# A recurrent mixer in which the token shift of V is given out behind Q

## The chip, the cores and the metric

The kernel runs on one core of a Trainium2 chip. Its time is the device time of one execution in microseconds. A core has five engines that run their own lists of instructions side by side: TensorE (PE, with PEld for its weight loads), VectorE (DVE), ScalarE (ACT), GpSimd (POOL) and SyncE (SP). Each engine takes its list strictly in order, and an instruction waits by semaphores for what other engines and DMAs have to deliver. DMAs are issued from SP and from ACT; in the profile such an issue has the engine's name with a q (SPq, ACTq).

## The reference

The model is a trunk of residual sub-layers over 256 tokens of width 1024: SwiGLU, mixer, SwiGLU, in two kinds of layer. The change lies in the first kind's mixer, whose recurrent half has 8 heads of 64. Cut to what the change touches:

```python
proj = h @ w_in
p = proj[..., :COLS_RWKV]
p_prev = jnp.pad(p, ((0, 0), (1, 0), (0, 0)))[:, :-1]
p = p + shift_mu * (p_prev - p)                 # token shift of r, k, v and the low-rank inputs
r, k, v, d_w, d_a, d_g = split_cols(p, [...])
w_log = -jax.nn.softplus(-(decay_base + jnp.tanh(d_w) @ decay_up)) - 0.5
decay = jnp.exp(-jnp.exp(w_log))
a = jax.nn.sigmoid(iclr_base + d_a @ iclr_up)
kk = k * k_k;  kk = kk * rsqrt(sum(kk * kk))    # per head
k = k * (1.0 + (a - 1.0) * k_a)
# S_t = S_{t-1} diag(w_t) - (S_{t-1} kk_t)(kk_t*a_t)^T + v_t k_t^T ;  y_t = S_t r_t
y = rwkv7_scan(r, decay, k, v, kk, a)
y = group_norm(y)                               # per head: mean and variance over 64
glu = c_val * jax.nn.sigmoid(c_gate)            # the other half: a convolution of 31 taps
return concat([(y + bonus) * g, silu(layer_norm(conv(glu)))]) @ w_out
```

## The kernel before, in words

The program is one core's list of stages: SwiGLU, the recurrent mixer, two SwiGLUs, an attention mixer, a SwiGLU. Tokens stand in two tiles of 128 (t = 0 and 1). All products with weights run in three passes: a page of weights (128x1024) is loaded by SP (`raw`, L68), ACT casts it to `whi` (L100), and VectorE, or GpSimd for some pages, subtracts to get `wlo` (L101). The product's three passes are the lines L340 and L354 on PE. SP loads pages ahead into a ring of 10 buffers, so a page's subtraction also frees a buffer for the next load.

The recurrent mixer is written as sub-steps, functions in a table `f`, that are called in the order of the string `ORDER` (L22), "VLDKPvQkRIBCcbA2S". A tile framework then puts the instructions on the engines, taking them by the order in which they were given out and by its own estimate of when they become ready; so the string moves what it names, and the framework moves neighbours. What the sub-steps are, with the names that the rows use:

- V (`values`): the product for V. ACT writes it to `pv` (L619) and copies it, shifted by one token, into `prev` by DMAs from ACT's queue (L622). v (`m["rest"]`, L628): the same for the second tile, and `shift_values`.
- `shift_values`: for each tile t, GpSimd mixes in the shifted token (L632, L633, L634, 128x512 each), VectorE sums over the 64 of each head and scales (L636, L637, written to the small tile `misc`), and GpSimd subtracts that mean (L640, `vz`, 64x512, two for each tile).
- L and D: the low-rank inputs (`lora`), the gates `sg` and `ic` (sigmoids on ACT), the decay scan on VectorE (L684, `dc`), then GpSimd's `epx` (L686) and ACT's exponentials `ep`, `epx` (L689, L687).
- K, P, k: k with its shift (`shifted`: VectorE L645 `n`, ACT L648, VectorE L649) and what is made of it, `bk` (L700, L703, L726) and `ur` (L697).
- Q (`qmats`): PE multiplies `ur` and `bk` head by head, and VectorE writes the masked and scaled result in 16 instructions (L740).
- I (`invert`): Q goes out to DRAM and comes back with another layout (DMAs L750, L756), VectorE inverts the small triangular blocks (L759, L760, then multiply L775, L778 and sum L780 in three rounds), and the inverse goes out and back (`dg`, `G`, L785, L788).
- R: r with its shift (L645, L648, L649), `ur` from r (L797), and GpSimd's `sq` (L803). C (`glu`): the gated value `cv` (L858), the gate `z` (L863 on VectorE, L864 on ACT), `glu` (L869, L871). A: products of r and k, `ak` and `ar` (L828, L831), behind which PE starts the sequential part (L590).

VectorE, GpSimd, ACT and SP keep their lists in the order that the framework chose; nothing overtakes.

Of the kernel before, what the change touches and what calls it, by code (L numbers as in the profile page):

```python
# [12 lines left out]
ALU = mybir.AluOpType  # L13
PSUM = bass.MemoryType.PSUM
P = 128
D = 1024
# [2 lines left out]
TAG = dict(sq8="y2", qn="yc", gz="z", fz="tmp", fe="c16", fl="lora", fc="n", fraw="restart", pt="yb", y="muv",  # L19
           cb="ur", cbm="bk", gt="sg", qt="ic", kt="k", v="vz", y0="ar")  # L20

ORDER = "VLDKPvQkRIBCcbA2S"  # L22

NRAW, NWEIGHT, NAHEAD = 10, 8, 8

# [69 lines left out]
class Kernel:  # L95
# [470 lines left out]
    def mixer_a(self, j, rstd, nxt, then):  # L566
        nc, W, a = self.nc, self.w, self.a
        V = nc.vector
# [15 lines left out]
        m = {}  # L584

        def abank():
            return self.abank(3 if m.get("busy") else 4)

        def mm(out, lhsT, rhs, start=True, stop=True):
            return nc.tensor.matmul(out, lhsT=lhsT, rhs=rhs, start=start, stop=stop, skip_group_check=True)  # L590
# [17 lines left out]
        def values():  # L608


            vz = m["vz"] = [half(self.page("vz")) for _ in range(2)]
            pv, prev = m["v"], _ = half(self.page("pv")), half(self.page("prev"))
            W.upto(("av",))
            with self.tc.issue_after(self.pow.ins):
                nc.gpsimd.memset(prev[0:1, 0, :], 0.0)

            def product(t):
                ps = self.xunit(("av",), t)
                nc.scalar.activation(pv[:, t, :], ps, AF.Copy, scale=rstd[t])  # L619

                for a, b in ((0, 112), (112, P - 1)):
                    nc.scalar.dma_start(out=prev[a + 1:b + 1, t, :], in_=pv[a:b, t, :])  # L622
                if t == 0:
                    nc.scalar.dma_start(out=prev[0:1, 1, :], in_=pv[P - 1:P, 0, :])

            product(0)
            m["rb"] = self.across(rstd)
            m["rest"] = lambda: (product(1), shift_values(vz, pv, prev))  # L628

        def shift_values(vz, pv, prev):  # L630
            for t in range(2):
                nc.gpsimd.tensor_tensor(out=prev[:, t, :], in0=prev[:, t, :], in1=pv[:, t, :], op=ALU.subtract)  # L632
                nc.gpsimd.tensor_tensor(out=prev[:, t, :], in0=prev[:, t, :], in1=muv, op=ALU.mult)  # L633
                nc.gpsimd.tensor_tensor(out=pv[:, t, :], in0=prev[:, t, :], in1=pv[:, t, :], op=ALU.add)  # L634
                v8 = self.small("v8", 8)
                V.tensor_reduce(out=v8, in_=h8(pv[:, t, :]), axis=AX.X, op=ALU.add)  # L636
                V.tensor_scalar(out=v8, in0=v8, scalar1=1.0 / 64, scalar2=None, op0=ALU.mult)  # L637
                for c in range(2):
                    cs = slice(64 * c, 64 * c + 64)
                    nc.gpsimd.tensor_tensor(out=h8(vz[t][cs, c, :]), in0=h8(pv[cs, t, :]), in1=v8[cs].unsqueeze(2).broadcast_to([64, 8, 64]), op=ALU.subtract)  # L640
# [87 lines left out]
        def qmats():  # L728
            Q = m["Q"] = blk(self.page("Q"))
            bk, ur, nn = m["bk"], m["ur"], m["nn"]  # L730
            for t in range(2):
                pss = [abank()[:, 0:256].rearrange("p (g x) -> p g x", x=64) for _ in range(2)]
                for g in range(4):
                    for c in range(2):
                        for hp in range(2):
                            b, o = 64 * hp, 64 * (c ^ hp)
                            z = 1 + (1 - (c ^ hp))
                            mm(pss[hp][o:o + 64, g, :], bk[g // 2][b:b + 64, g % 2, t, z, :], ur[g // 2][b:b + 64, g % 2, t, z, :])
                for h in range(8):
                    V.scalar_tensor_tensor(out=Q[:, t, h, :], in0=pss[h % 2][:, h // 2, :], scalar=nn[:, t, h:h + 1], in1=self.tri[:, 0:64], op0=ALU.mult, op1=ALU.mult)  # L740

        def invert():

# [238 lines left out]
        def state():  # L982
# [4 lines left out]
            for ch in range(4):  # L987
# [35 lines left out]
                if c == 1:  # L1023
# [11 lines left out]
                    ts = slice(t * P, (t + 1) * P)  # L1035
                    self.split(self.xth[:, 0:4, ts], self.xtl[0][:, :, ts], tp.rearrange("p (g t) -> p g t", t=P))

        f = {"V": values, "v": lambda: m["rest"](), "L": lora, "K": keys, "D": decay, "P": prep, "k": kprep, "Q": qmats, "I": invert, "R": receptance, "A": amats,
             "B": kback, "C": glu, "2": doubling, "b": bonus, "c": conv, "S": state}
        for z in ORDER:  # L1040
            f[z]()
# [9 lines left out]
    def plan(self, stages):  # L1051
        W, a = self.w, self.a
        flat = lambda ap: ap.rearrange("p k f -> p (k f)")
        for st in stages:
# [17 lines left out]
            if st == "A":  # L1072
                for name in [n for z in ORDER for n in dict(V=["alora", "av"], K=["ak"], R=["ar"], C=["acv", "acg"]).get(z, [])]:
                    if name == "av":
# [154 lines left out]
```

## Time and profile before

| | us |
|---|---|
| median of 3 runs | 1127.58 (1126.9 to 1128.02) |
| profiled execution, own time | 1126.15 |
| profiled execution, span of the core | 1124.4 |
| PE busy in the span | 1082.3 (96%) |
| VectorE busy | 657.7 (58%) |
| ACT busy | 545.7 (49%) |
| GpSimd busy | 232.7 (21%) |

The span is the stretch from the first to the last instruction of the profiled execution; 1.75 us of its own time lie around it. The recurrent mixer's sub-steps lie between about 205 and 370 us of the span. PE is busy nearly everywhere; behind the first of the page's 40 slices (28.1 us each) the lowest is the one of 281 to 309 us, with 7 tenths for PE and 7 for its clock. The granted clock stands as a share of TensorE's full speed.

### The profile page before, as it was taken

To read this page: it belongs to the slowest core of one execution; us is meant where nothing else is said; L and a number is where in the kernel's file an instruction comes from. 1 tells how busy PE (TensorE), PEld (TensorE's weight loads), DVE (VectorE), ACT (ScalarE), POOL (GpSimd) and SP (SyncE) were. 2 spreads that over 40 slices of the span, in tenths; PEclk is the share of its full clock that TensorE was granted. 3 is DMA by queue.
4 is the path that set the end of the run, shared out by engine and by line. 5 is a ranking of instruction groups with operands and counts; after the bars stand their busy time and mean duration, and the time that the engine had idled before them with its cause. 6 is when DMAs were issued, how large, how long until landed. Compare 5 with 4: busy or idle time off the path is not lost.

```text
span 1124.4 us, 17702 instructions
## 1 busy us (share of the span) xinstructions
PE 1082.3 (96%) x7021; PEld 950.2 (85%) x7021; DVE 657.7 (58%) x1041; ACT 545.7 (49%) x876; POOL 232.7 (21%) x164
## 2 busy tenths in 40 slices
PE   7999999999799899999989999999999989999997
PEld 5899988779688779999878999988887868999986
DVE  4565661598874566557444655836666665555722
ACT  7444543572302564446354544644666945444611
POOL 5200005454700160000070000001564541000000
PEclk9999999999799999999999999999999999999999
DMA  9766784155631146547455655734273563665400
GB/s 358 252 211 188 235 291 160 56 177 157 159 110 38 59 166 246 215 185 272 155 183 162 194 188 184 235 127 150 92 284 112 189 188 112 208 187 187 149 1 38
DMA packets 66633, 192.84 MB, mean 172 GB/s; under 512 B 18520, under 2 KB 20216, under 8 KB 66550
## 3 DMA queue, kind: packets, MB, share of 16 engines
q1 hardware_dynamic: 56698, 189.75, 50.7%
q10 hardware_dynamic: 9852, 1.96, 0.9%
q8 instruction: 55, 0.90, 0.3%
q14 instruction: 28, 0.23, 0.1%
HBM read 187.86 MB, written 2.92 MB: 170 GB/s over the span
## 4 chain that ended last, share of the span: by engine, by line
PE 88%; DVE 4%; ACT 3%; POOL 2%; DMA 2%; issue 1%; ACTq 0%; DVEq 0%; SPq 0%; POOLq 0%
PE gu L354 32%; PE acc L265 21%; PE gu L225 15%; PE gu L340 6%; PE acc L590 5%; PE acc L372 3%; PE gu L590 1%; DVE x L150 1%; DVE wlo L101 1%; PE tr L160 1%; POOL p L486 1%; PE tr L245 1%; ACT whi L100 1%; DMA raw<-in_wgt_dram 1%; PE tr L508 1%
## 5 line engine op out<-in xcount | busy, mean ns | idle before, releaser
L100 ACT CAST whi<-raw 128x1024 fp32r<-128x1024 f32 x294 | 302.2, 1047 | 212.8 <-PE gu L354 114.3
L101 DVE TENSOR_TENSOR wlo<-raw,whi 128x1024 fp32r<-128x1024 f32 x248 | 310.5, 1260 | 145.6 <-ACT whi L100 122.7
L354 PE MATMUL gu<-xth,whi 128*128 128x256 f32 x1104 | 313.5, 284 | 0.9 <-DVE misc L810 0.6
L354 PE MATMUL gu<-xth,wlo 128*128 128x256 f32 x1104 | 313.5, 284 | 0.0
L354 PE MATMUL gu<-xl,whi 128*128 128x256 f32 x1104 | 312.8, 284 | 0.0
L354 PEld LDWEIGHTS gu<-xth,whi 128*128 128x128 f32 x1104 | 212.2, 192 | 4.4 <-issue 0.8
L354 PEld LDWEIGHTS gu<-xth,wlo 128*128 128x128 f32 x1104 | 212.2, 192 | 2.4
L354 PEld LDWEIGHTS gu<-xl,whi 128*128 128x128 f32 x1104 | 212.1, 192 | 0.8 <-issue 0.7
L101 POOL TENSOR_TENSOR wlo<-raw,whi 128x1024 fp32r<-128x1024 f32 x46 | 112.2, 2466 | 311.5 <-PE gu L225 142.0
L265 PE MATMUL acc<-whi,ht 128*128 128x512 f32 x576 | 168.0, 393 | 0.0
L115 POOL TENSOR_TENSOR misc<-misc 128x1 f32<-128x1 f32 (+1 forms) x36 | 31.4, 872 | 484.4 <-DVE misc L132 382.3
L265 PEld LDWEIGHTS acc<-whi,ht 128*128 128x128 f32 x576 | 104.0, 189 | 18.3
L265 PE MATMUL acc<-wlo,ht 128*128 128x512 f32 x288 | 89.9, 392 | 0.0
L236 DVE TENSOR_TENSOR h<-gu,h 128x256 f32<-128x256 f32 x88 | 36.8, 419 | 77.7 <-ACT h L232 74.2
L225 PE MATMUL gu<-whi,xth 128*128 128x512 f32 x160 | 63.6, 401 | 1.6 <-ACT whi L100 1.6
L225 PE MATMUL gu<-wlo,xth 128*128 128x512 f32 x160 | 63.6, 399 | 0.5 <-DVE wlo L101 0.5
L265 PEld LDWEIGHTS acc<-wlo,ht 128*128 128x128 f32 x288 | 53.9, 188 | 11.8
L225 PE MATMUL gu<-whi,xl 128*128 128x512 f32 x160 | 63.4, 401 | 0.4 <-DVE xl L165 0.4
L234 DVE TENSOR_TENSOR h<-gu,misc 128x256 f32<-128x256 f32 x56 | 23.7, 423 | 65.7 <-PE gu L354 65.6
L232 ACT ACTIVATE h<-gu,misc 128x256 f32<-128x256 f32 x32 | 15.1, 474 | 73.1 <-PE gu L225 39.9
L340 PE MATMUL gu<-whi,xl 128*128 128x512 f32 x112 | 44.9, 401 | 1.1 <-DVE xl L165 0.9
L340 PE MATMUL gu<-whi,xth 128*128 128x512 f32 x112 | 45.1, 403 | 0.7 <-ACT xth L164 0.7
(259 smaller groups left out, 1521.0 us busy)
## 6 DMA issues: line engine op xcount, KB each, us to landing
raw<-in_wgc_dram SPq DMA_DIRECT2D x112, 512.0 KB, 4.3
raw<-in_wd_dram SPq DMA_DIRECT2D x88, 512.0 KB, 4.5
raw<-in_wgt_dram SPq DMA_DIRECT2D x64, 512.0 KB, 4.8
raw<-in_cin_dram SPq DMA_DIRECT2D x24, 512.0 KB, 4.6
raw<-in_ain_dram SPq DMA_DIRECT2D x18, 512.0 KB, 4.3
raw<-in_aout_dram SPq DMA_DIRECT2D x8, 512.0 KB, 4.9
raw<-in_cgate_dram SPq DMA_DIRECT2D x8, 512.0 KB, 4.7
raw<-in_cout_dram SPq DMA_DIRECT2D x8, 512.0 KB, 5.8
```

Of the source, the lines that this page charges most:

```text
L100: self.nc.scalar.copy(out=hi, in_=raw)
L101: (engine or self.nc.vector).tensor_tensor(out=lo, in0=raw, in1=hi.bitcast(F32), op=ALU.subtract)
L115: self.pow = self.nc.gpsimd.tensor_tensor(out=out, in0=v, in1=self.mhalf[:, :n], op=ALU.pow)
L225: nc.tensor.matmul(ps, lhsT=l, rhs=r[:, k % 2], start=n == 0, stop=n == 23)
L232: nc.scalar.activation(sl, ps[:, 0:256], AF.Silu, scale=rstd[u[2]])
L234: nc.vector.tensor_tensor(out=z, in0=ps[:, 0:256], in1=self.rb, op=ALU.mult)
L236: nc.vector.tensor_tensor(out=h, in0=ps[:, 256:512], in1=sl, op=ALU.mult)
L265: mm = nc.tensor.matmul(out, lhsT=l, rhs=r, start=u[1] == 0 and i + n == 0, stop=u[1] == NB - 1 and i * 3 + n == 5)
L340: self.nc.tensor.matmul(ps, lhsT=l, rhs=r[:, k % 2], start=n == 0, stop=n == 23)
L354: self.nc.tensor.matmul(ps[:, j * 256:(j + 1) * 256], lhsT=l, rhs=r, start=n == 0, stop=n == 23)
L372: self.nc.tensor.matmul(accs[t][c], lhsT=l, rhs=r[:, 0, c * 512:(c + 1) * 512], start=k == ks[0] and n == 0, stop=k == ks[7] and n == 2)
L590: return nc.tensor.matmul(out, lhsT=lhsT, rhs=rhs, start=start, stop=stop, skip_group_check=True)
```

## The change

A new letter s, the shift of V, comes behind Q in the order, and v keeps only the second tile's product with its DMAs. The shift is wrapped in `issue_after` on the last of VectorE's 16 operations for Q. That edge orders instructions of one engine only: VectorE's L636 and L637 of both tiles have to stand behind Q in VectorE's list, while GpSimd's list gets no such edge. From L634 on all line numbers rise by 5.

```diff
--- before.py
+++ after.py
@@ -19,7 +19,7 @@
 TAG = dict(sq8="y2", qn="yc", gz="z", fz="tmp", fe="c16", fl="lora", fc="n", fraw="restart", pt="yb", y="muv",
            cb="ur", cbm="bk", gt="sg", qt="ic", kt="k", v="vz", y0="ar")
 
-ORDER = "VLDKPvQkRIBCcbA2S"
+ORDER = "VLDKPvQskRIBCcbA2S"
 
 NRAW, NWEIGHT, NAHEAD = 10, 8, 8
 
@@ -625,9 +625,14 @@
 
             product(0)
             m["rb"] = self.across(rstd)
-            m["rest"] = lambda: (product(1), shift_values(vz, pv, prev))
+            m["rest"], m["shift"] = lambda: product(1), lambda: shift_values(vz, pv, prev)
 
         def shift_values(vz, pv, prev):
+
+            with self.tc.issue_after(m["last_q"].ins):
+                shift_behind(vz, pv, prev)
+
+        def shift_behind(vz, pv, prev):
             for t in range(2):
                 nc.gpsimd.tensor_tensor(out=prev[:, t, :], in0=prev[:, t, :], in1=pv[:, t, :], op=ALU.subtract)
                 nc.gpsimd.tensor_tensor(out=prev[:, t, :], in0=prev[:, t, :], in1=muv, op=ALU.mult)
@@ -737,7 +742,7 @@
                             z = 1 + (1 - (c ^ hp))
                             mm(pss[hp][o:o + 64, g, :], bk[g // 2][b:b + 64, g % 2, t, z, :], ur[g // 2][b:b + 64, g % 2, t, z, :])
                 for h in range(8):
-                    V.scalar_tensor_tensor(out=Q[:, t, h, :], in0=pss[h % 2][:, h // 2, :], scalar=nn[:, t, h:h + 1], in1=self.tri[:, 0:64], op0=ALU.mult, op1=ALU.mult)
+                    m["last_q"] = V.scalar_tensor_tensor(out=Q[:, t, h, :], in0=pss[h % 2][:, h // 2, :], scalar=nn[:, t, h:h + 1], in1=self.tri[:, 0:64], op0=ALU.mult, op1=ALU.mult)
 
         def invert():
 
@@ -1035,7 +1040,7 @@
                     ts = slice(t * P, (t + 1) * P)
                     self.split(self.xth[:, 0:4, ts], self.xtl[0][:, :, ts], tp.rearrange("p (g t) -> p g t", t=P))
 
-        f = {"V": values, "v": lambda: m["rest"](), "L": lora, "K": keys, "D": decay, "P": prep, "k": kprep, "Q": qmats, "I": invert, "R": receptance, "A": amats,
+        f = {"V": values, "v": lambda: m["rest"](), "s": lambda: m["shift"](), "L": lora, "K": keys, "D": decay, "P": prep, "k": kprep, "Q": qmats, "I": invert, "R": receptance, "A": amats,
              "B": kback, "C": glu, "2": doubling, "b": bonus, "c": conv, "S": state}
         for z in ORDER:
             f[z]()
```

VectorE, the stretch from `ur` to the first operations for Q. `ur<-k` and `bk` are what PE multiplies for Q, `tr` their sums of squares, `r` the start of sub-step R, `misc<-pv` the mean of V's second tile. Before:

```order
L697 SCALAR_TENSOR_TENSOR ur<-k,cst,epx 128x2x128 x4
L703 TENSOR_TENSOR bk<-bk,dc 128x4x128 x2
L101 TENSOR_TENSOR wlo<-raw,whi 128x1024
L722 TENSOR_TENSOR k<-k,ic 128x1024
L645 TENSOR_TENSOR n<-gu,misc 128x512
L101 TENSOR_TENSOR wlo<-raw,whi 128x1024 x2
L726 TENSOR_TENSOR bk<-k,dc 128x4x2x64 x2
L715 TENSOR_SCALAR misc<-tr 64x16 x2
L649 SCALAR_TENSOR_TENSOR r<-n,cst,r 128x255 x2
L636 TENSOR_REDUCE misc<-pv 128x8
L716 RECIPROCAL misc<-misc 128x16
L797 TENSOR_TENSOR ur<-r,ep 128x2x2x64 x2
```

The 16 operations of Q follow (with one L637 ahead of them and one `wlo` ahead of the last). Now:

```order
L702 SCALAR_TENSOR_TENSOR ur<-k,cst,epx 128x2x128 x4
L708 TENSOR_TENSOR bk<-bk,dc 128x4x128 x2
L720 TENSOR_SCALAR misc<-tr 64x16 x2
L727 TENSOR_TENSOR k<-k,ic 128x1024
L101 TENSOR_TENSOR wlo<-raw,whi 128x1024
L721 RECIPROCAL misc<-misc 128x16
L101 TENSOR_TENSOR wlo<-raw,whi 128x1024
L731 TENSOR_TENSOR bk<-k,dc 128x4x2x64 x2
L745 SCALAR_TENSOR_TENSOR Q<-acc_2377,misc,cst 128x64 x3
```

Gone from ahead of Q are not only the sum of V, but also `n`, `r` and `ur` of sub-step R, one `wlo` of three, and the `wlo` that stood inside Q.

VectorE again, from the last operations for Q to the first step of the inversion (`inv<-inv`), whose operand comes back from DRAM. Before:

```order
L101 TENSOR_TENSOR wlo<-raw,whi 128x1024
L740 SCALAR_TENSOR_TENSOR Q<-acc_2418,misc,cst 128x64
L645 TENSOR_TENSOR n<-gu,misc 128x512
L101 TENSOR_TENSOR wlo<-raw,whi 128x1024
L649 SCALAR_TENSOR_TENSOR r<-n,cst,r 128x255 x2
L797 TENSOR_TENSOR ur<-r,ep 128x2x2x64 x2
L101 TENSOR_TENSOR wlo<-raw,whi 128x1024
L858 TENSOR_TENSOR cv<-gu,misc 128x512
L101 TENSOR_TENSOR wlo<-raw,whi 128x1024
L759 TENSOR_TENSOR inv<-inv,c_2608 128x256
```

Now:

```order
L745 SCALAR_TENSOR_TENSOR Q<-acc_2404,misc,cst 128x64
L641 TENSOR_REDUCE misc<-pv 128x8 x2
L650 TENSOR_TENSOR n<-gu,misc 128x512
L101 TENSOR_TENSOR wlo<-raw,whi 128x1024
L642 TENSOR_SCALAR misc<-misc 128x8
L101 TENSOR_TENSOR wlo<-raw,whi 128x1024
L642 TENSOR_SCALAR misc<-misc 128x8
L654 SCALAR_TENSOR_TENSOR r<-n,cst,r 128x255 x2
L101 TENSOR_TENSOR wlo<-raw,whi 128x1024
L802 TENSOR_TENSOR ur<-r,ep 128x2x2x64
L764 TENSOR_TENSOR inv<-inv,c_2608 128x256
L650 TENSOR_TENSOR n<-gu,misc 128x512
```

Both sums of V stand directly behind Q. The first half of r stands between Q and the inversion, and r's second half (`n`, two L654, two L802), one L802 of the first half, both `cv` and four `wlo` now stand behind the inversion's first step, where one `cv` and two `wlo` stood.

GpSimd, from the shift of V's first tile to `sq`, before:

```order
L632 TENSOR_TENSOR prev<-prev,pv 128x512
L633 TENSOR_TENSOR prev<-prev,muv 128x512
L634 TENSOR_TENSOR pv<-prev,pv 128x512
L101 TENSOR_TENSOR wlo<-raw,whi 128x1024
L640 TENSOR_TENSOR vz<-pv,misc 64x512 x2
L101 TENSOR_TENSOR wlo<-raw,whi 128x1024 x5
L686 TENSOR_TENSOR epx<-dc,sg 128x1024
L632 TENSOR_TENSOR prev<-prev,pv 128x512
L633 TENSOR_TENSOR prev<-prev,muv 128x512
L634 TENSOR_TENSOR pv<-prev,pv 128x512
L640 TENSOR_TENSOR vz<-pv,misc 64x512 x2
L803 TENSOR_TENSOR sq<-r,k 128x1024
```

Now:

```order
L637 TENSOR_TENSOR prev<-prev,pv 128x512
L638 TENSOR_TENSOR prev<-prev,muv 128x512
L639 TENSOR_TENSOR pv<-prev,pv 128x512
L101 TENSOR_TENSOR wlo<-raw,whi 128x1024 x6
L691 TENSOR_TENSOR epx<-dc,sg 128x1024
L637 TENSOR_TENSOR prev<-prev,pv 128x512
L638 TENSOR_TENSOR prev<-prev,muv 128x512
L639 TENSOR_TENSOR pv<-prev,pv 128x512
L645 TENSOR_TENSOR vz<-pv,misc 64x512 x4
L808 TENSOR_TENSOR sq<-r,k 128x1024
```

GpSimd's three operations of each tile keep their places. The first tile's two `vz` moved behind the second tile's mixing, so that six `wlo` stand in one go and four `vz` stand ahead of `sq`.

Further moves without rows here: on VectorE the second half of k (`n`, L654, L705, L726) now stands ahead of the decay scan (L689), on ACT k's two L653 stand between the last sigmoids for the scan, and ACT's table load for `ep` stands directly behind them; on SP the two DMAs of Q (L755) stand ahead of the eighth load of the output projection's weights.

## Rows read from the trace of the kernel before

**Rows 1.** Page, part 1: busy time, share of the span, instructions

```profile
PE 1082.3 (96%) x7021; PEld 950.2 (85%) x7021; DVE 657.7 (58%) x1041; ACT 545.7 (49%) x876; POOL 232.7 (21%) x164
```

**Rows 2.** Stretches: PE, PEld, DVE, ACT, POOL busy (instructions), PEclk, DMA share, GB/s

```profile
250.00:255.00 5.00, 2.92 (x78) 2.50 (x80) 5.00 (x8) 1.92 (x3) 0.17 (x1) 1.00 0.48 172
...
280.00:300.00 20.00, 12.01 (x95) 10.75 (x94) 15.04 (x23) 8.79 (x11) 15.60 (x10) 0.84 0.56 129
```

**Rows 3.** Waits of 237 to 300 us: total us, times, longest

```profile
PE gu L590 <- DVE ak L828: 7.3, 1, 7.3
```

**Rows 4.** Chain of waits, 225 to 480 us: start, us, what

```profile
249.10 5.57 DMA prev<-pv
...
260.86 1.36 POOL pv L634
...
298.44 0.33 DVE ak L828
```

**Rows 5.** VectorE's timeline ahead of Q: start, us, line, operation xcount [idle <-releaser]

```profile
230.66 2.60 DVE L700 SCALAR_TENSOR_TENSOR bk<-k,cst,ic 128x256 f32<-128x256 f32 x1
...
238.55 2.28 DVE L684 TENSOR_TENSOR_SCAN dc<-restart,sg 128x1024 f32<-128x1024 bf16 x1
...
248.99 1.66 DVE L697 SCALAR_TENSOR_TENSOR ur<-k,cst,epx 128x256 f32<-128x256 f32 x4
...
254.05 0.68 DVE L645 TENSOR_TENSOR n<-gu,misc 128x512 f32<-128x512 f32 x1
254.65 2.35 DVE L101 TENSOR_TENSOR wlo<-raw,whi 128x1024 fp32r<-128x1024 f32 x2
...
258.50 2.56 DVE L649 SCALAR_TENSOR_TENSOR r<-n,cst,r 128x255 f32<-128x255 f32 x2
262.25 0.69 DVE L636 TENSOR_REDUCE misc<-pv 128x8 f32<-128x512 f32 x1 [1.19 <-POOL pv L634]
...
263.01 0.69 DVE L797 TENSOR_TENSOR ur<-r,ep 128x256 f32<-128x256 f32 x2
...
266.57 1.21 DVE L101 TENSOR_TENSOR wlo<-raw,whi 128x1024 fp32r<-128x1024 f32 x1
267.70 0.28 DVE L740 SCALAR_TENSOR_TENSOR Q<-acc,misc,cst 128x64 f32<-128x64 f32 x1
```

**Rows 6.** VectorE's timeline behind Q

```profile
269.62 0.87 DVE L649 SCALAR_TENSOR_TENSOR r<-n,cst,r 128x255 f32<-128x255 f32 x2
...
273.86 1.81 DVE L101 TENSOR_TENSOR wlo<-raw,whi 128x1024 fp32r<-128x1024 f32 x1 [0.96 <-ACT whi L100]
277.07 0.43 DVE L759 TENSOR_TENSOR inv<-inv,c 128x256 f32<-128x256 f32 x1 [1.40 <-DMA inv<-dq]
...
286.46 0.69 DVE L780 TENSOR_REDUCE inv<-tmp 128x64 f32<-128x512 f32 x1
```

**Rows 7.** GpSimd's timeline

```profile
216.25 1.29 POOL L632 TENSOR_TENSOR prev<-prev,pv 128x512 f32<-128x512 f32 x1 [7.89 <-ACT misc L388]
...
225.51 12.39 POOL L101 TENSOR_TENSOR wlo<-raw,whi 128x1024 fp32r<-128x1024 f32 x5
...
254.83 4.51 POOL L632 TENSOR_TENSOR prev<-prev,pv 128x512 f32<-128x512 f32 x1 [11.44 <-DMA prev<-pv]
...
263.95 2.14 POOL L640 TENSOR_TENSOR vz<-pv,misc 64x512 f32<-64x512 f32 x2 [1.74 <-PE gu L354]
270.67 3.92 POOL L803 TENSOR_TENSOR sq<-r,k 128x1024 f32<-128x1024 f32 x1 [4.58 <-DVE r L649]
```

**Rows 8.** ACT's timeline

```profile
237.69 1.28 ACT L689 ACT_TABLE_LOAD   x1
...
245.00 1.06 ACT L687 ACTIVATE epx<-epx 128x1024 f32<-128x1024 f32 x1
...
291.00 1.28 ACT L864 ACT_TABLE_LOAD   x1 [0.91 <-PE gu L354]
```

**Rows 9.** SP's timeline

```profile
268.00 1.36 SPq L750 DMA_DIRECT2D dq<-Q  x2
```

## The prediction

> **What bounds the kernel now.** The page's busy times come first. PE is busy for 96% of the span, VectorE for 58% [rows 1], so for most of the run only PE's own work counts. I then looked for the places where PE stands still, by stretches of some microseconds. In the recurrent mixer two stick out: 250 to 255 us, with 2.92 of 5 us busy, and 280 to 300 us, with 12.01 of 20 at a mean granted clock of 0.84 [rows 2]. The list of waits names the second: PE waits 7.3 us for `ak`, an operation of VectorE that ends at 298.8 us [rows 3, 4]. Behind it PE works almost without a gap, so the end of the kernel moves by what `ak` moves, as far as PE keeps that work.
>
> What sets `ak`? Followed back in VectorE's list: the gate (z, glu), ahead of it ACT's table load at 291.00 and the inverse's way out and back, which starts when the last L780 has ended at 287.15 [rows 6, 8]. The inversion's first step starts at 277.07 and had waited 1.40 us for Q to come back [rows 6]; Q leaves from SP at 268.00, straight after VectorE's last operation for Q at 267.98 [rows 5, 9]. And ahead of Q VectorE waited 1.19 us for GpSimd's mixing of V's second tile, whose operand had landed late: a DMA of 5.57 us from 249.10, then three GpSimd operations until 262.2 [rows 4, 5, 7]. So the chain is V's shift, Q, inversion, gate, `ak`. The change works on its first link.
>
> **The change, part by part.** I add three terms: when `ur` starts, how long VectorE then needs to Q's end, and how long from there to the last L780 (now L785). All times are those of the profiled execution, 1126.15 us of its own, 1.43 under the median of 1127.58; the sum is a difference and is applied to the median.
>
> *From `ur` to Q's end.* Before, 248.99 to 267.98, 19.0 us [rows 5]. In the new order these are no longer in it: `n` 0.68, one `wlo` of the pair (2.35 for two, so 1.18), the two operations for r 2.56, the wait 1.19, the sum of V 0.69, the first two `ur` of r 0.69, and the `wlo` inside Q 1.21. Together 8.2 us; neighbouring rows overlap by about 0.08 each, so I take 7.8 off. All of it stood in VectorE's list with nothing else under way there, so it counts in full: 11.2 us remain. PE's side follows: Q's products wait for `ur` and `bk` alone, which no longer stand behind anything new.
>
> *From Q's end to the last sum of the inversion.* Before, 267.98 to 287.15, 19.2 us: 9.1 to the inversion's first step, 10.1 from there on [rows 5, 6]. Ahead of the first step the new list has two sums of V (1.38), `n` 0.68, three `wlo` (3.63), two L642, two operations for r (0.87) and one `ur` (0.35). That is about 7, less overlaps 6.6. Q's way to DRAM and back lasts 9.1, so these hide beside it, and there is room of 2.5 us for a wait. One may come: the second sum needs GpSimd's last mixing operation. It ended at 262.2 before; now Q's end would be near 259.4, the sum would want to start near 260, and GpSimd's mixing, which has lost two `vz` and stands at the same place, ends somewhere from 259 to 262. A wait up to 2 us is covered by Q's way; above that it is paid.
>
> Behind the first step the list holds more than before: two further `wlo` (2.42), one `n` (0.68), three `ur` (1.04), one `cv`, of the same shape as `n` (0.68), and two operations for r (0.87) [rows 5, 6]. That is 5.7, less overlaps 5.1. None of it has cover: these stand between the steps of the inversion. Then GpSimd. Four `vz` and `sq` now run beside exactly these steps. In the trace an operation of VectorE beside `sq` (3.92 us) took 1.81 where its like takes 1.21 [rows 5 to 7]; two more `vz` of 1.07 each come to the same place. I take 1.1 for it; bounds are 0 and, if each of the four `vz` holds VectorE for half its time and `sq` for 1, about 3. So this term is +6.2, from +3.6 (Q comes back 1.5 us sooner, with no cost from GpSimd) to +8.
>
> *The start of `ur`.* The first sum of V and its scaling leave VectorE's list ahead of the low-rank inputs, and GpSimd's `wlo` run without the two `vz` between them, so their end, 237.9 us before (225.51 + 12.39) [rows 7], comes up to 2.8 us sooner. While they run, VectorE is held: an operation like the first `bk` takes 2.60 there [rows 5]. Against that, k's second half now stands ahead of the decay scan, and the scan ran at 238.55 before, right at the end of GpSimd's row of `wlo`. I work the scan out at 241 to 242, its exponentials (`epx`, 245.00 before) 1.3 to 2 later, because ACT's table load of 1.28 [rows 8] was done beside the scan and is now behind it. But k's second half, `bk` and its rest, 2 to 3 us of VectorE by rows of the same shapes, is then already done, where before it stood between scan and `ur`. Bounds for `ur`: 2.0 sooner, if VectorE gets in between GpSimd's operations, to 0.5 later, if `epx` decides. I take 0.8 sooner.
>
> The Trainium skill ("SBUF — State Buffer", section "SBUF: two separate sides") says that VectorE and GpSimd take a shared pair of ports as an exclusive lock for a whole instruction, and that the other one fully blocks. This trace agrees: GpSimd's first mixing operation takes 4.51 us beside a busy VectorE and 1.29 without [rows 7]. By that rule alone, with no gap left between six `wlo`, the start of `ur` would go as in the second rival below.
>
> *Sum:* -0.8 - 7.8 + 6.2 = -2.4 us. Behind that nothing in the order has changed in kind: the table load, z, glu and `ak` move with the inverse. PE's hole of 7.3 us stays about as long, since PE's work ahead of it also waits for VectorE; its low clock stays with it. The DMAs of Q on SP now stand ahead of one more weight load, which costs nothing: that load waited for GpSimd in any case and its page is for the output projection, 80 us later. So 1127.58 - 2.4 = **1125.2 us**; the likeliest case's own range takes the ends of the terms: -2.0 - 7.8 + 3.6 = -6.2 and 0.5 - 7.8 + 8 = +0.7, and since not all ends come together, 1122.6 to 1127.4.
>
> **Rivals.**
>
> *The wait only moves (same).* The second sum now stands directly behind Q, ahead of r and of every step of the inversion. If GpSimd's mixing ends at 264 instead of 262, because V's product now stands behind all of k's on PE and so its DMA of 5.57 us leaves up to 2 us later, the sum waits 4 and 2 of them are paid. For it: GpSimd was the chain's last link before [rows 4]. Against: Q's way of 9.1 us covers most. Price: -2.4 + 2 = -0.4, 1127.2.
>
> *The scan becomes the late one (slower).* Six `wlo` in one go hold VectorE, ACT's last sigmoids stand behind k's second half, which waits for VectorE, and the scan waits for the sigmoids. If two more of VectorE's operations there are held for 2.4 us each, scan, table load, `epx` and `ur` come 4.8 later than I take them: -2.4 + 4.8 = +2.4, 1130.0. It decides from the point where `epx` on ACT ends behind 249, `ur`'s start before. For it: the first `bk` took 2.60 beside GpSimd's row, about one of its five `wlo` (12.39 / 5 = 2.48) [rows 5, 7], so VectorE got through one operation for each of GpSimd's. Against: GpSimd also starts its row sooner.
>
> *Q's gain goes through (faster by more).* If the extra operations behind the inversion's first step fall into VectorE's waits, and Q's way is short, the term behind Q shrinks to about +2 and the sum is -6.6, 1121.0. The order speaks against: they stand between dependent steps in a list that keeps its order.
>
> *The change doesn't hold V back.* The edge binds VectorE alone, and GpSimd's list has the second tile's mixing where it was. But the order shows both sums behind Q, so VectorE's wait ahead of Q is gone.
>
> **How the numbers follow.** The measurement can tell about 0.2%, 2.26 us, from no change. The forecast's case has 62%; its middle lies on that bound, so I give 36 of it to faster and 26 to same. The wait that moves has 12%, 10 to same and 2 to slower. The late scan has 15%, all slower. The large gain has 11%, all faster. That makes faster 0.47, same 0.36, slower 0.17. The range from 1121.5 to 1129.3 reaches nearly to both outer cases.
>
> **What would show it.** In the new profile: no wait for GpSimd ahead of VectorE's first operation for Q, and about 11 us from `ur` to Q's end; from Q's end to the last L785 24 to 26 us; `sq` and the four `vz` beside slow operations of VectorE; `ak` and PE's restart some 2 us sooner than 298.8. It would be wrong if `ur` starts behind 250, if PE's hole ahead of `ak` changes its length by more than 1 us, or if the time moves at a place outside 215 to 300 us, such as the end of the mixer, where the framework also exchanged GpSimd's and PE's operations and where I take no gain or loss.

## The result and the profile after

The changed kernel takes 1140.07 us (median of 4 runs, 1139.03 to 1140.28) against 1127.8 for the kernel before on the same chip (4 runs, 1126.9 to 1129.56). The ratio is 1.0108, interval 1.0096 to 1.012: it is slower by 12.3 us, where 1125.2 was forecast, and outside the range.

The page's busy times, as [rows 1] were for before (the span is 1138.5 us, before's was 1124.4):

```profile
PE 1092.6 (96%) x7021; PEld 956.5 (84%) x7021; DVE 656.2 (58%) x1041; ACT 546.7 (48%) x876; POOL 236.9 (21%) x164
```

All engines have the instructions that they had. PE is busy for 10.3 us longer, GpSimd for 4.2 and ACT for 1.0: on PE, which bounds the kernel, the same products ran slower somewhere. Landmarks of both profiled executions, in us from the span's start, show where it is. The third column is a second profile of the changed kernel, from the run called after_again.

| | before | after | after again |
|---|---|---|---|
| `n` of the low-rank inputs starts | 222.60 | 222.91 | 220.52 |
| decay scan starts | 238.55 | 243.19 | 240.79 |
| `ur` starts | 248.99 | 251.69 | 249.29 |
| Q's end | 267.98 | 262.72 | 260.32 |
| first step of the inversion starts | 277.07 | 272.81 | 271.77 |
| last sum of the inversion ends | 287.15 | 290.32 | 289.25 |
| first `ak` ends | 298.77 | 302.31 | 301.24 |
| first product of T and Q | 315.02 | 323.07 | 321.99 |
| first product of the output projection | 366.66 | 377.23 | 376.80 |
| span | 1124.4 | 1138.5 | 1138.3 |

Three places make up the 14 us: 3.5 (2.5 in the second profile) have come up by `ak`, 7.0 (7.7) more between `ak` and the output projection, and the rest lies far behind, in the attention stage. "After" carries 2.4 us from 215 us on that the second profile does not have: 0.8 from the program's start, and the rest from a stretch of 3.4 us at half clock at 208 us. So the second profile is the better one up to `ur`. The profiled execution of before (1126.15 us) is 1.65 faster than the median of 1127.8, so the medians lie 12.3 us apart where the profiles lie 14.

**VectorE.** Its timeline after, to be held against [rows 5, 6]:

```profile
251.69 1.66 DVE L702 SCALAR_TENSOR_TENSOR ur<-k,cst,epx 128x256 f32<-128x256 f32 x4
...
259.57 3.15 DVE L745 SCALAR_TENSOR_TENSOR Q<-acc,misc,cst 128x64 f32<-128x64 f32 x16
262.65 0.67 DVE L641 TENSOR_REDUCE misc<-pv 128x8 f32<-128x512 f32 x1
263.59 0.69 DVE L641 TENSOR_REDUCE misc<-pv 128x8 f32<-128x512 f32 x1 [0.28 <-POOL pv L639]
...
265.92 0.17 DVE L642 TENSOR_SCALAR misc<-misc 128x8 f32<-128x8 f32 x1
266.00 1.22 DVE L101 TENSOR_TENSOR wlo<-raw,whi 128x1024 fp32r<-128x1024 f32 x1
267.13 1.02 DVE L642 TENSOR_SCALAR misc<-misc 128x8 f32<-128x8 f32 x1
268.06 1.66 DVE L654 SCALAR_TENSOR_TENSOR r<-n,cst,r 128x255 f32<-128x255 f32 x2
269.64 2.06 DVE L101 TENSOR_TENSOR wlo<-raw,whi 128x1024 fp32r<-128x1024 f32 x1
271.63 1.26 DVE L802 TENSOR_TENSOR ur<-r,ep 128x256 f32<-128x256 f32 x1
272.81 0.41 DVE L764 TENSOR_TENSOR inv<-inv,c 128x256 f32<-128x256 f32 x1
...
279.40 2.95 DVE L101 TENSOR_TENSOR wlo<-raw,whi 128x1024 fp32r<-128x1024 f32 x1 [0.30 <-ACT whi L100]
...
289.63 0.69 DVE L785 TENSOR_REDUCE inv<-tmp 128x64 f32<-128x512 f32 x1
```

In the second profile the first step waits for Q's return:

```profile
271.77 0.42 DVE L764 TENSOR_TENSOR inv<-inv,c 128x256 f32<-128x256 f32 x1 [1.28 <-DMA inv<-dq]
```

GpSimd in the first profile, as [rows 7] before:

```profile
266.23 6.37 POOL L645 TENSOR_TENSOR vz<-pv,misc 64x512 f32<-64x512 f32 x4 [2.68 <-DVE misc L642]
277.16 4.11 POOL L808 TENSOR_TENSOR sq<-r,k 128x1024 f32<-128x1024 f32 x1 [4.55 <-DVE r L654]
```

The wait for GpSimd ahead of Q is gone, and from `ur` to Q's end it takes 11.0 us. But from Q's end to the last sum it takes 27.6, where it took 19.2. Together 38.6, where it was 38.2: what left the first stretch came up in the second. Beside the four `vz` a scaling of 128x8 takes 1.02 for 0.17, the pair for r 1.66 for 0.87, a `wlo` 2.06 for 1.22; beside `sq` a `wlo` takes 2.95. Not every operation there is slower: the `wlo` at 266.00, beside the first `vz`, takes its usual 1.22.

The Trainium skill ("SBUF — State Buffer", section "SBUF: two separate sides") says that a VectorE operation with two SBUF inputs, or in a two-port mode, and a GpSimd operation take a shared pair of ports as a lock for a whole instruction, and that whichever starts first blocks the other. The trace agrees in that either engine is held: the `wlo` of 2.06 us, with two inputs, is 0.84 longer than usual, and GpSimd's four `vz` take 6.37 us, where the two pairs took 2.23 and 2.14 before.

**PE behind `ak`.** Stretches of 10 us, columns as in [rows 2]. Before:

```profile
290.00:300.00 10.00, 2.71 (x20) 1.83 (x20) 6.98 (x9) 5.22 (x7) 10.00 (x7) 0.67 0.63 131
300.00:310.00 10.00, 10.00 (x45) 8.74 (x46) 9.62 (x16) 0.00 (x0) 5.07 (x4) 0.50 0.71 212
310.00:320.00 10.00, 10.00 (x146) 8.40 (x145) 6.95 (x16) 0.47 (x1) 0.11 (x1) 0.98 0.36 125
320.00:330.00 10.00, 10.00 (x164) 7.87 (x161) 8.37 (x17) 1.05 (x2) 0.11 (x1) 1.00 0.16 55
```

After:

```profile
290.00:300.00 10.00, 7.24 (x66) 6.91 (x64) 5.41 (x6) 6.13 (x7) 10.00 (x7) 1.00 0.65 112
300.00:310.00 10.00, 8.01 (x29) 5.64 (x30) 9.72 (x15) 0.63 (x1) 7.27 (x5) 0.53 0.54 157
310.00:320.00 10.00, 10.00 (x48) 8.31 (x48) 4.47 (x12) 0.00 (x0) 0.00 (x0) 0.50 0.36 113
320.00:330.00 10.00, 10.00 (x122) 7.91 (x121) 6.26 (x14) 0.47 (x1) 0.11 (x1) 0.78 0.33 107
```

Read the last column but two, the granted clock. 0.50 is 1.2 GHz, 1.00 is 2.4. In both kernels the clock falls in PE's hole ahead of `ak`, which lasts 7.29 us before and 4.75 after. Before, the clock is back at 310.4 us, 11.6 us after PE restarts; after, only at 324.5, 22.5 us after the restart. At half clock work takes almost twice its time: four records of the convolution (128x244) took 1.09 us before, at 314.01, and 1.99 after, at 321.16. So 10.9 us more of it cost about 5 us; I take half, 5.4, as an estimate. What PE does there, before (start, us, operation, count, wait ahead of it):

```profile
298.82 0.47 PE L590 MATMUL gu<-vz,ak 64*64 64x64 f32 x2 [7.29 <-DVE ak L828]
...
305.45 0.47 PE L590 MATMUL gu<-vz,ak 64*64 64x64 f32 x2
305.85 2.07 PE L590 MATMUL acc<-ur,bk 64*128 64x128 f32 x8
307.85 4.09 PE L590 MATMUL acc<-glu,raw 128*128 128x256 f32 x12
...
314.01 1.09 PE L590 MATMUL acc<-glu,raw 128*128 128x244 f32 x4
```

And after:

```profile
301.99 2.04 PE L590 MATMUL acc<-glu,raw 128*128 128x256 f32 x4 [4.75 <-DVE z L868]
303.96 0.47 PE L590 MATMUL gu<-vz,ak 64*64 64x64 f32 x2
...
304.91 2.08 PE L590 MATMUL acc<-ur,bk 64*128 64x128 f32 x8
306.91 2.04 PE L590 MATMUL acc<-glu,raw 128*128 128x252 f32 x4
308.88 1.75 PE L590 MATMUL gu<-vz,ak 64*64 64x64 f32 x14
310.56 3.09 PE L590 MATMUL acc<-ur,bk 64*128 64x128 f32 x16
313.58 0.47 PE L590 MATMUL gu<-vz,ak 64*64 64x64 f32 x2
313.98 2.01 PE L590 MATMUL acc<-glu,raw 128*128 128x248 f32 x4
```

`acc<-glu,raw` is the convolution, which `pfeed` gives out between the chunks of `amats`, two products for each chunk. Before, the framework put six of them (12 records) in one row, and the clock came back inside that row. After, the same products stand in pairs between products that use 64 of the 128 rows of TensorE (64\*128 and 64\*64 in the rows, against 128\*128), and the clock stayed low. One pair now stands ahead of the first product with `ak`. The hole is shorter mainly because PE's work ahead of it ends at 297.24 for 291.54, later by more than `ak` is. The change names none of these instructions.

**The attention stage.** From 544 to 774 us of before's span the second profile of after stays 10.5 to 10.8 us behind, by the starts of the same products; from 816 on it is 13.8 behind. The order of PE's products between is the same, but one long wait is new. After, PE's product for v, and ACT's timeline ahead of it:

```profile
822.63 0.65 PE L340 MATMUL gu<-whi,xth 128*128 128x512 f32 x1 [1.61 <-ACT v L425]
```

```profile
818.00 1.28 ACT L446 ACT_TABLE_LOAD   x1
...
819.73 1.28 ACT L447 ACT_TABLE_LOAD   x1
...
821.92 0.66 ACT L425 ACTIVATE v<-gu,misc 128x512 f32<-128x512 f32 x1
```

The `gu` tiles rotate through two PSUM buffers. After, this tile got the buffer that ACT's copy of v still holds, and that copy stands behind two table loads. Before, the same product starts at 810.01, while that copy runs only from 810.96, and it does not wait. Behind the gap the clock is low for 3.4 us from 823, another 1.7.

The sum for "after": 3.5 by `ak`, 5.4 at half clock behind it, 1.6 and 1.7 in the attention stage, and 1.7 for a stretch of 3.4 us at half clock at 369 us, which before does not have. That is 13.9 of the 14.1 between the two profiles. Of the 3.5, the second profile has only 2.5.

### The profile page after: what moved, and what is told of

Same layout as the page of the kernel before. It is cut to its first block, busy times and chain, and to the rows that moved or that the text cites. A ratio compares the mean times of both kernels' runs of the same rounds, so it can differ in the third digit from the quotient of the medians.

```text
span 1138.5 us, 17699 instructions
## 1 busy us (share of the span) xinstructions
PE 1092.6 (96%) x7021; PEld 956.5 (84%) x7021; DVE 656.2 (58%) x1041; ACT 546.7 (48%) x876; POOL 236.9 (21%) x164
## 4 chain that ended last, share of the span: by engine, by line
PE 67%; DVE 4%; ACT 2%; DMA 1%; POOL 1%; issue 1%; ACTq 0%; DVEq 0%; POOLq 0%
PE gu L354 23%; PE acc L265 16%; PE gu L225 12%; PE acc L590 5%; PE gu L340 4%; PE acc L372 3%; PE gu L590 1%; DVE x L150 1%; POOL p L486 1%; PE tr L160 1%; DVE wlo L101 1%; PE tr L508 1%; PE acc L495 0%; PE tr L245 0%; DMA raw<-in_wd_dram 0%
## 5 line engine op out<-in xcount | busy, mean ns | idle before, releaser
L101 DVE TENSOR_TENSOR wlo<-raw,whi 128x1024 fp32r<-128x1024 f32 x248 | 310.4, 1258 | 153.8 <-ACT whi L100 130.2
```

Of the source, the lines that this page charges most:

```text
L101: (engine or self.nc.vector).tensor_tensor(out=lo, in0=raw, in1=hi.bitcast(F32), op=ALU.subtract)
```

## The experiments

The theory: the loss is mostly PE's clock behind `ak`, kept low by the place of the convolution's products. The rival: VectorE's longer way to `ak` explains it. Ratios are against the kernel before, run on the same chip.

**The changed kernel again,** unchanged.

> The changed kernel once more, for a second profile. The first shows 12 us more in the median; 0.8 of it by VectorE's chain up to ak, 5.4 by a longer stretch of half clock behind ak (300.6 to 324.5 us against 293.3 to 310.4), the rest in short dips of the clock and a late first load. If these short dips belong to the order, this profile shows them again at 208, 369 and 823 us. If they are chance, they stand elsewhere or are gone, while the long stretch is there again, about 24 us long. Time in both cases 1138 to 1141.

Measured: 1140.29 us, ratio 1.0107 (1.0091 to 1.0123). The loss repeats, and so do the 23.9 us at half clock behind `ak`, the gap in the attention stage and its dip, and the dip at 369 us. The one at 208 does not, and others stand at 253 and 270: these come and go between profiles of one kernel.

**After, convolution in one row.**

```diff
-                pfeed(PFEED[0], i)
+                pfeed((0, 0, 6, 2)[ch], i)
```

> The changed kernel, but PE's first six products of the convolution stand in one go behind the third chunk of ur-bk products, as in the kernel before, instead of in pairs behind each chunk. Theory (the order of PE's work behind ak keeps the clock low): half clock behind ak ends after 10 to 13 us of work instead of 22, time about 1134 to 1136. Rival (the clock and the loss come from ak's being late and from PE's longer hole ahead of it): half clock stays at about 24 us and the time at 1139 to 1141.

Measured: 1135.65 us, ratio 1.0059 (1.0044 to 1.0074). Stretches:

```profile
300.00:310.00 10.00, 6.61 (x33) 5.51 (x33) 9.71 (x14) 1.36 (x2) 8.29 (x6) 0.52 0.54 157
310.00:320.00 10.00, 10.00 (x50) 8.15 (x50) 5.27 (x13) 0.00 (x0) 0.00 (x0) 0.63 0.46 131
320.00:330.00 10.00, 10.00 (x190) 8.30 (x191) 8.43 (x19) 0.94 (x2) 0.21 (x2) 1.00 0.33 108
```

```profile
312.42 5.25 PE L590 MATMUL acc<-glu,raw 128*128 128x256 f32 x12
```

The half clock ends at 317.4, inside the row of six (312.42 to 317.67), and 14.0 us behind PE's restart at 303.39, where 10 to 13 were expected. It lasts 17.1 us in all, as in before, instead of 23.9. `ak` ends at 303.33, later than in after, and the kernel is still 4.6 us faster. Some 3.4 of that is the shorter half clock; 1.7 more is the dip at 823, which this profile does not have, though it has the gap of 1.6. So the place of these products holds 3 to 5 us, and VectorE does not explain them.

**Before, convolution in pairs.** The other way round: every later product of `ur` and `bk` has to stand behind the pair given out ahead of it.

```diff
-                        i = mm(pss[hp][:, g, :], both(bk, g, t, c)[b], both(ur, g, t, c)[b])
+                        with self.tc.issue_after(m["lastp"].ins) if ch else contextlib.nullcontext(): i = mm(pss[hp][:, g, :], both(bk, g, t, c)[b], both(ur, g, t, c)[b])
...
-                    mm(o[:, 2 * s:256], w, m["glu"][j % 2][:, j // 2, 0:256 - 2 * s], s == 0, s == 7)
+                    m["lastp"] = mm(o[:, 2 * s:256], w, m["glu"][j % 2][:, j // 2, 0:256 - 2 * s], s == 0, s == 7)
```

> The kernel before, but PE's first eight products of the convolution are held in pairs between the four chunks of ur-bk products, as in the changed kernel. VectorE's shift of V stays ahead of Q. Theory: half clock behind ak gets longer by 7 us or more, time 1131 to 1134. Rival: the clock comes back as before (about 11.6 us after PE's restart) and the time stays within 2 us of before, 1126 to 1130.

Measured: 1138.07 us, ratio 1.0076 (1.0049 to 1.0104). Stretches:

```profile
300.00:310.00 10.00, 9.17 (x38) 7.18 (x39) 9.81 (x14) 0.63 (x1) 7.49 (x5) 0.50 0.68 192
310.00:320.00 10.00, 10.00 (x40) 7.82 (x40) 4.06 (x11) 0.00 (x0) 0.00 (x0) 0.50 0.21 71
320.00:330.00 10.00, 10.00 (x98) 8.10 (x99) 6.57 (x15) 0.47 (x1) 0.11 (x1) 0.63 0.36 107
```

Half clock for 30.7 us, with V's shift where it always was, and with VectorE's three stretches as in before (19.0, 8.9 and 10.1 us from `ur` to the last sum). The time lies above the forecast of 1131 to 1134, and its four runs spread from 1133.2 to 1139.8. This kernel's hole is also longer, 8.9 us, and ends with the convolution's input; that is part of its loss. So the direction is shown from both sides, the size not exactly.

**Only the second tile's shift moved.** The first tile's goes back into `m["rest"]`; the lines that hand `shift_behind` its tiles are left out here.

```diff
-            m["rest"], m["shift"] = lambda: product(1), lambda: shift_values(vz, pv, prev)
+            m["rest"], m["shift"] = lambda: (product(1), shift_behind(vz, pv, prev, (0,))), lambda: shift_values(vz, pv, prev)
```

> The changed kernel, but only the second tile's shift of V stands behind Q; the first tile's is given out with its product, as before. GpSimd's list is then as before up to sq, r's first half stays ahead of Q on VectorE, and PE's six products of the convolution stand in one go. From ur to Q's end 19.0 less the wait 1.2, the sum 0.7 and the wlo 1.2: about 16 us; behind Q the sum and one wlo are added. Theory (two causes, GpSimd beside the inversion and the clock, are both gone): ak within 1 us of 298.8 and the time 1125 to 1129. Rival (any sum of V behind Q costs the inversion its place): ak 2 us or more late, time 1130 or more.

Measured: 1130.63 us, ratio 1.0023 (1.001 to 1.0036). The scan is back at 238.87 and the row of six is whole. From `ur` to Q's end 16.9 us, from there to the last sum 20.8: 37.7 together, 0.5 under before. `ak` ends at 299.46, 0.7 us later than before, as the theory had it; the median lies in the rival's range. What left the first stretch is partly a wait now: VectorE waits 3.28 us for Q's return, where it waited 1.40. The profiled execution (1127.71) is the fastest of eight, so it does not show what the slower ones lose. Nothing is gained here either.

**Zero products in the hole, before and after.** 28 (18 in after) products of zeros stand in PE's hole ahead of `ak`, with the convolution in one row. The edit in both, with the edges that hold the later products behind the zeros left out here:

```diff
+                if ch == 0:
+                    with self.tc.issue_after(i.ins):
+                        for _ in range(28):
+                            m["warm"] = mm(m["pconv"].rearrange("p i t -> p (i t)"), self.zb[:, 0:P], self.zb)
+                pfeed((0, 0, 6, 2)[ch], i)
```

> The kernel before, with 28 products of zeros (bf16, 128x512, into a PSUM bank that nothing reads before it is written anew) put on PE into the hole ahead of ak, and six products of the convolution in one go as before. Nothing of the computation is left out. Theory (the hole lets the granted clock fall, and PE's work behind ak then runs at half clock): no half clock from 293 to 310 us, 5 to 6 us gained, time 1121 to 1124. Rival (the clock falls for another reason, or PE's work behind ak waits for VectorE anyway): within 2 us of before, 1126 to 1130, or more if the zeros stand in ak's way.

> The changed kernel with the convolution's six products in one go and 18 such products of zeros ahead of ak. Theory: the clock's part of the loss is gone altogether, what is left is ak's 2 to 3 us and the wait in the attention stage (1.6 us and what its clock dip adds): 1129 to 1132, and 6 to 9 us above before_warm. Rival (the zeros change nothing): as after_group, 1134 to 1136.

Measured: before_warm 1132.02 us, ratio 1.0034 (1.0023 to 1.0044); after_warm 1133.12, 1.0041 (1.0029 to 1.0053). Both forecasts failed. In before_warm the clock holds until 300.7, but then PE waits again and the clock falls for 13.7 us. PE's waits in before_warm, 285 to 312 us (us in total, times, longest):

```profile
PE gu L590 <- DVE ak L833: 4.9, 1, 4.9
PE acc L590 <- DVE ar L836: 1.0, 1, 1.0
```

So PE behind `ak` depends on VectorE's next operations too; a faster clock there waits. after_warm was forecast at 1129 to 1132 and 6 to 9 us above before_warm; it stands 1.1 above it. Its half clock behind `ak` is 10.2 us instead of the 17.1 of after_group, but against after_group the ratio fell by only 0.0018, 2 us, and this kernel also has no gap in the attention stage. So the zeros do not tell what the clock costs.

**After, convolution in one row, without the subtraction of V's mean.** It leaves that subtraction out: zeros written at the start stand for `vz`.

```diff
-                    nc.gpsimd.tensor_tensor(out=h8(vz[t][cs, c, :]), in0=h8(pv[cs, t, :]), in1=v8[cs].unsqueeze(2).broadcast_to([64, 8, 64]), op=ALU.subtract)
+                    nc.gpsimd.memset(vz[t][cs, c, :], 0.0)
```

> As after_group, but the four vz are filled with zeros at the program's start instead of computed: leaves out the subtraction of V's mean, so GpSimd has no vz beside VectorE's steps behind Q. Theory (GpSimd's vz hold VectorE there, 2 to 3.5 us in all): from Q's end to the last sum of the inversion 25 to 26.5 us instead of 28.7, ak 2 to 3 us sooner, time 1132 to 1133. Rival (VectorE's own longer list sets it): 28 us or more, time 1134 to 1136.

Measured: 1125.83 us, ratio 0.9983 (0.9973 to 0.9992). But the stretch that it was made for did not shrink: Q's end to the last sum is still 28.5 us. Ahead of the inversion's first step VectorE now waits 1.95 us for Q's return, and behind it the operations beside `sq` and the gate's weights (`Wg`) are the slow ones. The kernel is faster since its whole chain runs earlier (`ur` at 244.29), and it has no gap in the attention stage: taking the four `vz` out also changed GpSimd's order ahead of the scan and VectorE's order ahead of Q (16.4 us from `ur` to Q's end). So taking `vz` out did not shorten the second stretch; since the lists changed with it, the run does not price `vz` alone.

**Before, all eight convolution products at the first chunk.**

```diff
-                pfeed(PFEED[0], i)
+                pfeed((8, 0, 0, 0)[ch], i)
```

> The kernel before, with eight products of the convolution in one go behind the first chunk's edge instead of six and two. Theory (long products in one go bring the clock back): half clock behind ak ends as soon as before or up to 2 us sooner, time 1125 to 1128. Rival (the number in one go says nothing): 1126 to 1130.

Measured: 1129.15 us, ratio 1.001 (1.0001 to 1.002). 17.1 us at half clock, as before, and the time lies in the rival's range: a row that is two products longer brings nothing here.

**The buffer, in before.** One more tile of the pair `gu` and one small product into it, at the start of the attention stage.

```diff
+        spare = self.bank("gu", 2)
+        self.nc.tensor.matmul(spare[0:2, 0:2], lhsT=self.ident[:, 0:2], rhs=self.ident[:, 0:2], start=True, stop=True)
```

> The kernel before with one more tile of the pair of PSUM buffers named gu and one product of 2x2 into it, at the start of the attention stage; nothing reads it. It makes the second product for v there follow on the other buffer of the pair, as in the kernel after: its first L340 then waits for ACT's v L425, which stands behind two table loads. Theory (the gap at 822 us after is the buffer's): a gap of 1.6 us near 811 us, nothing else; 1127.8 + 1.6 = 1129.4, and up to 1131.1 if the clock falls behind it. Rival (the gap comes from another thing that the change moved): no gap, 1127.8.

Measured: 1131.58 us, ratio 1.0033 (1.0022 to 1.0044), 3.7 us over before. PE at that place, and the stretch around it:

```profile
815.31 0.50 PE L340 MATMUL gu<-whi,xth 128*128 128x512 f32 x1 [1.61 <-ACT v L428]
```

```profile
815.00:820.00 5.00, 4.69 (x14) 3.70 (x15) 2.73 (x6) 2.25 (x3) 0.00 (x0) 0.66 0.45 146
```

The same gap of 1.61, and behind it the same dip: 3.4 us at half clock from 816.1. One product of 2x2 in a kernel without the change brings both, 3.3 us by the profile and 2.5 to 5.0 by the ratio's interval. That the buffer brings the gap is shown. The dip is not sure to follow: after_group has the same gap and none behind it.

**The buffer, in after with the convolution in one row.** The same two lines ahead of the forget gate's products put the tile on its old buffer.

> The kernel after with the convolution's products grouped as in after_group, and one more tile of the pair gu with one product of 2x2 into it, given out ahead of the forget gate's products in the attention stage; it puts the second product for v back on the buffer that it has before. Theory: the gap of 1.6 us goes, the rest is after_group; 1135.6 - 1.6 = 1134.0, or 1132.3 where the dip of the clock behind it goes too. Rival (the gap is not the buffer's): 1135.6.

Measured: 1130.15 us, ratio 1.0024 (1.0014 to 1.0034). The gap is gone: PE is busy without a break from 805 to 830 us. The ratio fell by 0.0035, some 4 us, where 1.6 were expected, or 3.3 with the dip. The profile has 13.7 us at half clock behind `ak`, not 17.1, and no dip near 365 us, which the extra product, 500 us later, can hardly have set; I count 1.6 as shown and leave the rest open. With the row and the buffer both put back, 1.0024 is left, 2.7 us (1.6 to 3.8), and `ak` ends at 301.35, 2.6 later than before: what is left is about what VectorE's chain costs.

**The shift of V behind the inversion**, with the convolution in one row.

```diff
-ORDER = "VLDKPvQskRIBCcbA2S"
+ORDER = "VLDKPvQkRIsBCcbA2S"
...
-            with self.tc.issue_after(m["last_q"].ins):
+            with self.tc.issue_after(m["last_i"].ins):
...
-                    V.tensor_reduce(out=dst, in_=tm, axis=AX.X, op=ALU.add)
+                    m["last_i"] = V.tensor_reduce(out=dst, in_=tm, axis=AX.X, op=ALU.add)
```

> The kernel after with the shift of V behind the inversion's last sum instead of behind Q's last operation (the letter s behind I), and the convolution's products grouped as in after_group. Theory (behind Q the shift costs its own 1.7 us of VectorE and some 3.4 us by which GpSimd's four vz slow VectorE's operations beside them): Q's end about 11 us behind ur as in after, Q's end to the inversion's last sum 28.3 - 5.1 = 23 us, so the last sum 1 to 3.5 us ahead of the kernel before's 287.15, the sums of V in VectorE's idle time while the inverse is under way, ak 1 to 3.5 us ahead of 298.8, half clock behind it 17 us as before: 1124 to 1127. Rival A (what VectorE saves it waits for instead, Q's way back or ACT): the last sum stays near 287, 1127.8. Rival B (vz, now behind the last sum on GpSimd and behind the gate's weights, comes after ak): PE's hole ends with a wait for GpSimd, 1129 to 1132.

Measured: 1133.3 us, ratio 1.0047 (1.0035 to 1.0059). VectorE's timeline:

```profile
271.50 0.42 DVE L764 TENSOR_TENSOR inv<-inv,c 128x256 f32<-128x256 f32 x1 [4.73 <-DMA inv<-dq]
...
272.57 3.36 DVE L101 TENSOR_TENSOR wlo<-raw,whi 128x1024 fp32r<-128x1024 f32 x1
...
287.54 2.22 DVE L783 TENSOR_TENSOR tmp<-inv 128x512 f32<-128x512 f32 x1
289.79 0.69 DVE L785 TENSOR_REDUCE inv<-tmp 128x64 f32<-128x512 f32 x1
```

The theory failed, and the time lies above both rivals' ranges. The first rival's mechanism shows: with V's operations out of the stretch, VectorE waits 4.7 us for Q to come back, and then needs 19.0 us, not 10.1, since the framework left four `wlo` and half of r behind the first step and `sq` and `Wg` run beside them. The last sum ends at 290.47. The long second stretch is not V's shift alone: it is that VectorE reaches Q sooner, Q's return does not keep up, and a list that keeps its order does the passed-over work between the dependent steps. The second rival shows in part too: PE's hole ends with a wait of 3.6 us for GpSimd.

The chain's row for that return, in the same profile (start, us), against the time from issue to landing before:

```profile
263.88 7.59 DMA inv<-dq
```

```profile
inv<-dq ACTq DMA_DIRECT2D x1, 128.0 KB, 4.6
```

The return takes 3.0 us longer for the same 128 KB. In the second profile of after it is issued at 263.88 too, and VectorE has it at 271.77. SP's loads of weight pages run beside it in either kernel, at other moments; that these are the reason was not tried.

## Why the prediction was wrong

- *What bounds it, and Q's stretch: right.* `ur` to Q's end came to 11.0 us for 11.2. The wait for GpSimd ahead of Q is gone, and the second sum of V waits 0.28, inside the bound of 2. The rival "the wait only moves" did not come.
- *The start of `ur`: missed.* -0.8 was taken, bounds -2.0 to +0.5; it was +0.3 in the second profile. The low-rank inputs come 2.1 sooner, but GpSimd's row of `wlo`, which was to end "up to 2.8 us sooner", ends at 237.77 for 237.90, because it waits 2.2 us in its midst for ACT's `whi`. From the low-rank inputs to the scan it takes 20.3 us for 15.95, since k's second half with ACT's part now stands between. The scan at 240.79 is no later than the 241 to 242 worked out, and `epx` on ACT ends at 247.94, so the rival of the late scan did not come. But from scan to `ur` VectorE still has an operation of 2.50 us beside GpSimd's `epx` (`ic`, 0.41 elsewhere) and three `wlo`, so that way is only 1.9 shorter.
- *Q's end to the last sum: mis-sized.* +6.2 was taken, bounds +3.6 to +8; it was +8.4, and +9.8 in the second profile. The first step starts 10.1 (11.5) us behind Q's end, not 9.1. In the first profile VectorE's own list ahead of it sets that: the four `vz` ran there (266.23 to 272.60), not behind the first step as I had read the order, and beside them the list took 10.1 us for the 6.6 that I had added up. In the second profile Q's return sets it, which I had taken as a constant that does not depend on when it starts. Behind the first step it took 17.5 us instead of 16.3, with one `wlo` at 2.95 beside `sq`.
- *The sum.* So `ak` came 2.5 us later, not 2.4 sooner. VectorE had only 3.6 us of waits between `ur` and the last sum (1.19, 0.96 and 1.40 in [rows 5, 6]). Work that stays between the two points could win back only these waits and what GpSimd holds; the longer way of Q and the operations beside GpSimd took more.
- *The step that failed most* is the stretch behind `ak`, which the sum puts at nothing: "Behind that nothing in the order has changed in kind", and "its low clock stays with it". The engine's order behind `ak` had changed: the convolution's row of six was in pairs. I had looked at the three places the diff speaks of and not at PE's list behind the hole. Half clock lasted 22.5 us of work, not 11.6, about 5.4 us by the estimate above; after_group takes 4.6 of the loss away, 3.4 of it by the clock, and before_pairs brings the loss into a kernel without the change. The hole did not keep its length either: it shrank from 7.29 to 4.75 us, past the 1 us that the prediction named as a sign against it.
- *The time moved outside 215 to 300 us,* which the prediction named as a sign against it, but priced at nothing: a rotating buffer 550 us later gave 1.6 us and, with the dip behind it, 3.3, shown by before_slot. What sets the dip between 365 and 382 us, in six of the thirteen profiles, stays open, and so does why Q's return takes longer.

No kernel that computes the whole beats the kernel before; the nearest, before_first, stands at 1.001.

## What to carry to other kernels

Where a list between two points is full, moving work inside it can win little more than the waits in it (3.6 of 38.2 us here); sum these first. After a reordering, read the order of the engine that bounds the kernel to the end of the program, not only where the diff speaks: a framework may split a row of full-width products, or shift a rotating buffer, far from the edit. Behind a hole of TensorE, look at what stands next in its list: here that decided whether the low clock lasted 11.6 us of work or 22.5.

## What the runs showed of the hardware

- The stretch at half clock around PE's hole ahead of `ak` (3 to 9 us long) lasted from 10.2 to 30.7 us over the runs, with different work behind the hole. In a row of 12 full-size matmuls the clock came back after some 2.5 us (before) and 5 us (after_group). With the same matmuls in pairs it came back only 22.5 us behind the restart, with PE busy throughout.
- A gap of 1.6 us on PE, in the midst of full-size products, was followed by 3.4 us at half clock in three profiles of two kernels (after, after_again, before_slot), and in after_group by none; a gap of 1.68 us in before, at 376.25, was followed by none either.
- A VectorE operation on 128x8 elements took 1.02 us beside GpSimd's `vz`, six times the 0.17 that it took at 265.92.
- The same read of 128 KB out of DRAM took 4.6 us in one schedule (before) and 7.6 in another (after_late).
